# Moving the down projections' residual gain work into the up projections of a two-layer trunk

## The chip, the core and the metric

The kernel runs on one core of a Trainium2 chip. The metric is the device time of one execution in microseconds. A core has five engines, each with a queue that it works through in order: TensorE (PE, matmuls; its weight loads are shown as PEld), VectorE (DVE), ScalarE (ACT), GpSimd (POOL) and SyncE (SP), which here does nothing but issue DMAs. ACT and POOL issue some DMAs too. Engines wait for each other and for DMAs through semaphores, and so does the issue of a DMA: an entry in SP's queue whose buffer is not free yet holds up all entries behind it.

## The reference

All is float32, one sequence of 1024 rows, model width 1024, two layers. Layer 0's mixer is a gated delta net, layer 1's is retention. A layer is

```python
y = mixers[i](x * (1.0 + sc1) + sh1)
x = layer_norm(DN_ALPHA * x + (1.0 + g1) * y, ln_g[i, 0], ln_b[i, 0])
y = conv_ffn(x * (1.0 + sc2) + sh2, ffn_up[i], ffn_conv_w[i], ffn_conv_b[i], ffn_down[i])
x = layer_norm(DN_ALPHA * x + (1.0 + g2) * y, ln_g[i, 1], ln_b[i, 1])
```

with `conv_ffn` = (silu(causal conv of width 3 over `h @ up_gate`) * (`h @ up_value`)) @ `ffn_down`, hidden width 2816. The vectors sh, sc, g come from `e @ ada_w[i] + ada_b[i]`, e being a projection of the condition.

What matters here is the `x` in the fourth line. It is the normalized row times `ln_g[i, 0]` plus `ln_b[i, 0]`. The kernel stores the third line's rows without this scale and shift, since the matmul path folds them into its own scale and shift (`fold`), and applies them apart for the residual of the fourth line: one multiply and one add over each of 8 row tiles of 128 x 1024.

## The kernel before

**Matmuls.** Each float32 matmul is done as three passes on split operands (high and low part, `split`, lines 89 and 90: ACT makes the high part, DVE subtracts to get the low part; for a few tiles POOL subtracts). The large products use Strassen-Winograd with seven block products (`strassen` for the up projections, `proj_gen` for layer 1's output projection and for both down projections). An FFN runs so: the up projection's two first items with ordinary products (`side`), in between `build_T` and its `rest` make the sums and differences of input blocks on DVE; then 20 items by `wino`, each with seven products whose weight blocks DVE combines (L1217) and splits; two weight loads per item (L1223, L1224) into two `wr` buffers. Gate and value meet in `conv` and `gated` (L1563 to L1582), POOL makes four sums per pair of tiles (L1589), and SP stores them (L1573). The down projection then goes through seven products of eleven blocks each; per block SP loads one activation block (`ar`, L1274) and one weight block (`Br`, `Bw`, L1307), ACT and DVE split both. Its products p are, in this order: 11, S1 T1, S2 T2, S4 22, 12 21, S3 T3, 22 T4.

**Background work.** `bg_step` runs queued units (twice per `wino` item, once per down projection block): the `ada_w` vectors (`bg_ada`: a load `mvw` at L215, then DVE's L225 and L227), and `bg_gain`, which does the scale and shift for the residual of layer 1's mixer output on POOL (L397, L398) during retention.

**The residual of the down projections.** Layer i's rows after the mixer lie in DRAM as `xs[0]` and `xs[2]`, stored by ACT's queue (`ln_store`, L374). In `proj_gen`, four row tiles of the first half are loaded (`xload`, L284) during product p = 2, and DVE multiplies and adds in place (L1357, four operations of 128 x 512 per tile). For the second half, `gain_half` runs eight times during p = 3 and 4: SP loads 128 x 512 of a row tile into one of two `xT` buffers (L1347), POOL multiplies and adds (L1349), and POOL's own queue stores the result to DRAM, `xg[i + 1]` (L1350). These rows come back with `xload` before the last product. The scale and shift rows are broadcast over 128 partitions by `gain_rows` into four of the eight `auh` buffers, which later hold retention's `trig` tables (L1636).

**What sets the order.** The program is written as a stream and put in order per engine when it is built, by a planner that simulates a time line and starts an operation as soon as its data and buffers allow, earlier written ones first among those that are ready. A few loads are pinned with `after(...)` to be issued behind an anchor load. So a unit's place in the source is the latest point more than the only one.

Of the kernel before, what the change touches and what calls it, by code (L numbers as in the profile page):

```python
# [12 lines left out]
ALU = mybir.AluOpType  # L13
AX = mybir.AxisListType

P = 128
# [3 lines left out]
HALF = 512  # L20
# [13 lines left out]
def trunk_kernel(ctx: ExitStack, tc, A):  # L34
# [79 lines left out]
    bg, pend = [], []  # L114
# [4 lines left out]
    def bg_step(tile=mm_tile):  # L119
        bg_ps[0] = tile  # L120
        for p in pend:
            p[0] -= 1
        while pend and (pend[0][0] <= 0 or not bg):
            pend.pop(0)[1]()
            if not bg:
                break
        if bg:
            nxt = bg.pop(0)()
            if nxt:
                pend.append(list(nxt))  # L130

    def gemm_feat(src, hT_, step=True):
        w = load_w(src)
# [244 lines left out]

    xg = [dr.tile([S, D], F32, tag=f"xg{i}", name=f"xg{i}") for i in range(3)]

    def bg_gain(n, src, dst):
        gb = []

        def unit(c, r):
            if r == 0:
                gb[:] = [tl("auh", [P, HALF], name="gb") for _ in range(2)]
                for t, nm in zip(gb, ("ln_g", "ln_b")):
                    sp.dma_start(t, A[nm][n:n + 1, hs(c)].to_broadcast([P, HALF]))
            x = tl("lane", [P, HALF], name="xg")
            rs = slice(r * P, r * P + P)  # L390
            sp.dma_start(x, src[rs, hs(c)])
            if r == 7:
                return gain(x, rs, c)
            return 1, lambda: gain(x, rs, c)

        def gain(x, rs, c):
            pool.tensor_tensor(x, x, gb[0], ALU.mult)  # L397
            pool.tensor_tensor(x, x, gb[1], ALU.add)  # L398
            sp.dma_start(dst[rs, hs(c)], x)

        for c in range(2):
            for r in range(8):
                bg.append(lambda c=c, r=r: unit(c, r))

    def ln_hooks(half, xts, tag, vecs2, out, dst, key, npool=0):
        def build(f):
# [754 lines left out]
    def strassen(hT0, xts, scale, shift, items, tags=("hTb", "hTb", "qkv", "qkv", "aux"), direct=False):  # L1161
        B = {"11": hT0[:4], "21": hT0[4:]}
        nblk = [0]
        nacc = [0]

        def mm_on(*a, **kw):
            return pe.matmul(*a, skip_group_check=True, **kw)  # L1167

        held = {}

        def side(n, s):
            out = []
            for u in items[n][:2]:
                w = held.pop(u.offset, None) or load_w(u)
                if n == 0 and s == 0:
                    held[u.offset] = w
                X = acc_tile()
                for i, b in enumerate((("11", "21"), ("12", "22"))[s]):
                    for k in range(4):
                        mm3(X, w, k + 4 * i, B[b][k], i == 0 and k == 0, i == 1 and k == 3)  # L1180
                out.append(X)
            return out

        ahead, sinks = {}, {}
        for n in (1, 0):
            X = side(n, 0)
            if direct:
                sinks[n] = items[n][2]()
                for i in range(2):
                    sinks[n](2 * i, X[i], None)  # L1190
                continue
            ahead[n] = [tl("cv", [P, 516], name="ah")[:, 0:HALF] for _ in range(2)]
            for t, x in zip(ahead[n], X):
                act.activation(t, x, AF.Copy)
        rest = build_T(B, xts, scale, shift, tags)

        def block(src):
            n = nblk[0]
            nblk[0] += 1
            t = tl(("wh", "wl")[n % 2], [P, 2, HALF], F32R, name="wb")  # L1200
            split(t[:, 0], t[:, 1], src)
            return kn(t[:, 0]), kn(t[:, 1])

        def prod(src, b, onto=None):
            w = block(src)
            if onto is None:
                nacc[0] += 1
                acc = (acc_tile, acc_tile, sc_tile)[nacc[0] % 3]()
            else:
                acc = onto  # L1210
            for k in range(4):
                mm3(acc, w, k, B[b][k], onto is None and k == 0, k == 3, mm_on if onto is not None else pe.matmul)
            return acc

        def psub(x, y, op=ALU.subtract):
            t = mm_tile()
            dve.tensor_tensor(t, x, y, op)  # L1217
            return t

        def wino(n, sink):  # L1220
            ua, ub = items[n][:2]
            wa, wb = tl("wr", [P, D]), tl("wr", [P, D])
            sp.dma_start(wa, ua)  # L1223
            sp.dma_start(wb, ub)  # L1224
            a11, a12, a21, a22 = wa[:, hs(0)], wa[:, hs(1)], wb[:, hs(0)], wb[:, hs(1)]
            def copy_of(X, tag="cv"):
                t = tl(tag, [P, 516] if tag == "cv" else [P, HALF], name="pc")[:, 0:HALF]
                act.activation(t, X, AF.Copy)  # L1228
                return t

            X = prod(a11, "11")
            p1 = copy_of(X)
            s1 = psub(a21, a22, ALU.add)
            sink(0, prod(a12, "21"), p1)
            s2 = psub(s1, a11)
            Z = prod(s1, "T1")
            z5 = copy_of(Z)
            s4 = psub(a12, s2)
            prod(s2, "T2", X)
            u2 = copy_of(X)  # L1240
            s3 = psub(a11, a21)
            prod(s4, "22", Z)
            sink(1, Z, u2)
            bg_step()
            prod(s3, "T3", X)
            u3 = copy_of(X, "t2")
            sink(3, X, z5)
            sink(2, prod(a22, "T4"), u3)
            bg_step()

        bg_tag[0] = "lane"
        for n in range(2):
            if not direct:
                sinks[n] = items[n][2]()
                for i in range(2):
                    sinks[n](2 * i, ahead[n][i], None)
            X = side(n, 1)
            for i in range(2):
                sinks[n](2 * i + 1, X[i], None)
            if n == 0:  # L1260
                rest()
            if items[n][3]:
                items[n][3]()
        for n in range(2, len(items)):
            wino(n, items[n][2]())
            if items[n][3]:
                items[n][3]()
        bg_tag[0] = "wr"
        return B
# [5 lines left out]
            return raw  # L1275
        return ablk

    def proj_gen(nj, ablk, wsrc, slots, xsrc, G, final, ln_next, tag, ltags, dst, key, mm=pe.matmul, gate=None, gain=None):
        bal = {nm: BAL[ltags[4] + nm] for nm in ABLK + ("w11", "w21", "w22", "wT1", "wT2", "wT3", "wT4", "n", "h")}
        pa = [tl("aux", [P, 2, HALF], name="pa") for _ in range(4)]  # L1280
        p1 = [pa[t // 2][:, t % 2] for t in range(4)]
# [56 lines left out]

        xts = [[], []]
        stats = [[], []]  # L1340
        grows = gain_rows(gain[0], key) if gain else None

        def gain_half(n):
            hf, rs = n // 4, slice(HALF + n % 4 * P, HALF + (n % 4 + 1) * P)
            x = tl("xT", [P, HALF], name="xg")
            with after("w"):
                sp.dma_start(x, gain[1][rs, hs(hf)])  # L1347
            for r, op in zip(grows, (ALU.mult, ALU.add)):
                pool.tensor_tensor(x, x, r[hf], op)  # L1349
            pool.dma_start(xsrc[rs, hs(hf)], x)  # L1350

        def xload(half, t):
            xt = load_row(xsrc if half or not gain else gain[1], half, t)
            if half == 0 and gain:
                for r, op in zip(grows, (ALU.mult, ALU.add)):
                    for hf in range(2):
                        dve.tensor_tensor(xt[:, hs(hf)], xt[:, hs(hf)], r[hf], op)  # L1357
            xts[half].append(xt)
            stats[half].append(tl("st", [P, 2, 6]))

        def finish(half, t, nh, c):
# [89 lines left out]
        for p, (an, bn, fin, side, fresh) in enumerate(prods):  # L1451
# [8 lines left out]
            for j in range(nj):  # L1460
# [5 lines left out]
                with after("a"):  # L1466
                    for st in steps[p * nj + j + ahead:p * nj + j + ahead + 1]:
                        load_b(*st)
                if gain and p in (3, 4) and j % 2 == 0 and j < 8:
                    gain_half((p - 3) * 4 + j // 2)  # L1470
                if gain and p == 2 and j % 2 == 0 and j < 8:
                    xload(0, j // 2)
                if p == 2 and j < 4 and gate:
                    xload(0, j)
# [44 lines left out]
    def layer_tail(i, mix, wout, xsrc, x_mid, x_out, ln_next, final):  # L1519
# [11 lines left out]
        else:  # L1531
            mix.append((sc2, sh2))
            hT0, xts = proj_st(mix[0])
        bg_ada(i, 5, "row")
        if i == 0:
            for j in (1, 0, 4, 3):
                bg_ada(1, j, "col")
# [5 lines left out]
        def pair_items(fp):  # L1543
# [31 lines left out]
            def up_start():  # L1575
                seen = []

                def gated(q, a, b):
# [7 lines left out]
                    if len(seen) == 4:  # L1586
# [6 lines left out]
            return [(up[4 * fp], up[4 * fp + 2], gate_start, conv), (up[4 * fp + 1], up[4 * fp + 3], up_start, None)]  # L1593

        strassen(hT0, xts, sc2, sh2, [it for fp in range(NF // 2) for it in pair_items(fp)])
        slots = {"c": "hTa", "x": "qkv"}
        gb2 = gain_rows(3, ("mid", i), "hTb") if final else None
        return proj_st(proj_gen(NF // 2, ablk_of(ad, "qkv"), A["ffn_down"][i], slots, xg[i + 1], rows[i, 5],
                       (gb2, x_out) if final else None, ln_next, "hTb", ("hTb", "hTa", 8, 6, "f") if final else ("qkv", "hTa", 8, 4, "0"), x_out, ("out", i), gain=(2 * i, x_mid)))

    g1 = two("auh", F32, "g1")
    for nh in range(2):
# [355 lines left out]
```

## Time and profile before

| | |
|---|---|
| runs | 2961.66, 2965.21, 2967.01 us; median 2965.21 |
| profiled execution | 2955.5 us; its span 2953.7 us |
| mean granted TensorE clock | 0.984 |
| busy share | PE 95%, PEld 78%, DVE 76%, ACT 45%, POOL 15% |
| layer 0: mixer output projection ends, up projection begins | about 747 us |
| layer 0: up projection to down projection | about 1200 us |
| layer 1: mixer output projection ends, up projection begins | about 2275 us |
| layer 1: up projection to down projection | about 2727 us |

In a row of a group: line of the kernel, engine, operation, what is written <- what is read, shape, count, then total busy us and mean ns of one, then idle us of the engine just before and what ended it. In a row of a timeline: start and duration in us, engine (with q for its queue: issuing a DMA), line, operation, tiles, count; in brackets the idle time of the engine before it and what ended it. In a row of stretches: from:to and length, then busy us and count per engine, granted clock, DMA share and GB/s.

### The profile page before, as it was taken

What the parts mean: (1) busy time and instruction counts of PE and PEld (TensorE: products, weight loads), DVE (VectorE), ACT (ScalarE), POOL (GpSimd) and SP (SyncE); (2) the same over time, 40 slices, a digit from 0 to 9 for tenths busy, and PEclk for the clock granted to TensorE, in tenths of its full rate; (3) what the DMA queues carried; (4) which work ended last, traced back from release to release, by engine and by line L of the source; (5) the groups of instructions that cost most, each with busy time, mean ns of one, the idle gap of its engine ahead of it and who ended that gap; (6) DMA issues with size and microseconds to landing.
All of it is one profiled execution on the core that took longest, in us unless ns stands there. A gap on an engine that the chain in (4) does not pass through costs nothing.

```text
span 2953.7 us, 38896 instructions
## 1 busy us (share of the span) xinstructions
PE 2816.4 (95%) x13638; PEld 2303.2 (78%) x13638; DVE 2243.3 (76%) x4005; ACT 1318.0 (45%) x2413; POOL 451.1 (15%) x469
## 2 busy tenths in 40 slices
PE   8998898999999999999999999999999899999997
PEld 7887777887788888877878877777777788888885
DVE  5788787656688888968676756666689787777989
ACT  4745565444544444545333333222244544445443
POOL 0302221100001111140000022422202011111211
PEclk9999999999999999999999999999999999999999
DMA  7231222254244445765343364755654343324763
GB/s 277 86 111 65 83 79 80 83 168 158 92 160 163 150 162 174 286 225 175 131 147 121 109 229 144 222 169 177 198 204 146 103 136 107 107 102 159 278 205 136
DMA packets 244403, 451.01 MB, mean 153 GB/s; under 512 B 23088, under 2 KB 76592, under 8 KB 244208
## 3 DMA queue, kind: packets, MB, share of 16 engines
q1 hardware_dynamic: 213088, 401.07, 41.1%
q10 hardware_dynamic: 29760, 43.00, 4.0%
q0 software_dynamic: 1360, 4.46, 0.4%
q8 instruction: 107, 1.75, 0.2%
q14 instruction: 88, 0.72, 0.1%
HBM read 339.91 MB, written 108.53 MB: 152 GB/s over the span
## 4 chain that ended last, share of the span: by engine, by line
PE 77%; DVE 9%; DMA 6%; ACT 4%; issue 2%; POOL 1%; SPq 0%; POOLq 0%; ACTq 0%; DVEq 0%
PE acc L655 15%; PE acc L1167 10%; PE acc L110 6%; PE acc L111 6%; PE acc L112 6%; PE sc L1167 5%; PE acc L1441 4%; PE sc L655 4%; PE mm L655 2%; PE sc L111 2%; PE sc L112 2%; PE sc L110 2%; PE mm L658 1%; DMA Br<-in_ffn_down 1%; PE acc L314 1%
## 5 line engine op out<-in xcount | busy, mean ns | idle before, releaser
L655 PE MATMUL acc<-hT,wh 128*128 128x512 f32 x960 | 300.1, 394 | 0.0
L1441 PE MATMUL acc<-bb,ab 128*128 128x512 f32 x984 | 233.4, 395 | 9.7 <-DVE bb L90 7.0
L1589 POOL TENSOR_TENSOR o<-o 128x512 f32<-128x512 f32 x80 | 112.3, 1414 | 793.6 <-DVE o L1582 494.0
L1441 PEld LDWEIGHTS acc<-bb,ab 128*128 128x128 f32 x984 | 183.7, 189 | 54.0 <-DVE bb L90 11.8
L1167 PE MATMUL acc<-T,wb 128*128 128x512 f32 x840 | 202.9, 390 | 6.5 <-DVE wb L90 6.5
L655 PEld LDWEIGHTS acc<-hT,wh 128*128 128x128 f32 x960 | 182.2, 190 | 34.1
L89 ACT ACTIVATE ab<-ar 128x512 fp32r<-128x512 f32 x210 | 130.4, 627 | 174.1 <-PE mm L291 57.4
L655 PE MATMUL acc<-hT,wl 128*128 128x512 f32 x480 | 201.2, 419 | 0.0
L1167 PEld LDWEIGHTS acc<-T,wb 128*128 128x128 f32 x840 | 157.0, 188 | 42.9 <-DVE wb L90 9.8
L90 DVE TENSOR_TENSOR wl<-wr,wh 128x1024 fp32r<-128x1024 f32 x95 | 123.3, 1298 | 81.9 <-ACT wh L89 81.6
L90 DVE TENSOR_TENSOR ab<-ar,ab 128x512 fp32r<-128x512 f32 x210 | 159.7, 765 | 30.0 <-ACT ab L89 29.9
L90 DVE TENSOR_TENSOR wb<-mm,wb 128x512 fp32r<-128x512 f32 x216 | 146.0, 684 | 26.4 <-ACT wb L89 25.5
L89 ACT ACTIVATE wh<-wr 128x1024 fp32r<-128x1024 f32 x95 | 100.8, 1062 | 142.8 <-PE acc L655 66.4
L90 DVE TENSOR_TENSOR wb<-wr,wb 128x512 fp32r<-128x512 f32 x162 | 110.5, 687 | 69.0 <-ACT wb L89 68.8
L1228 ACT ACTIVATE pc<-acc 128x512 f32<-128x512 f32 x143 | 84.9, 594 | 163.1 <-PE acc L1167 108.8
L1568 DVE SCALAR_TENSOR_TENSOR o<-g,vc,o 128x512 f32<-128x512 f32 (+2 forms) x176 | 145.6, 844 | 6.2 <-ACT o L1563 5.5
L89 ACT ACTIVATE wb<-mm 128x512 fp32r<-128x512 f32 x216 | 123.9, 595 | 53.8 <-DVE mm L1217 49.3
L89 ACT ACTIVATE wb<-wr 128x512 fp32r<-128x512 f32 x162 | 99.8, 629 | 99.7 <-DMA wr<-in_ffn_up 36.4
L655 PE MATMUL acc<-wh,hT 128*128 128x512 f32 x384 | 137.4, 420 | 2.9 <-DVE vv L90 1.7
L110 PE MATMUL acc<-T,wb 128*128 128x512 f32 x292 | 115.6, 396 | 9.4 <-DVE wb L90 9.4
L476 DVE SCALAR_TENSOR_TENSOR qkv<-raw,vc,qkv 128x512 f32<-128x512 f32 x144 | 111.7, 780 | 11.4 <-ACT qkv L474 10.7
L111 PE MATMUL acc<-T,wb 128*128 128x512 f32 x292 | 115.1, 394 | 0.0
(641 smaller groups left out, 7428.6 us busy)
## 6 DMA issues: line engine op xcount, KB each, us to landing
wr<-in_ffn_up SPq DMA_DIRECT2D x92, 512.0 KB, 4.2
mvw<-in_ada_w SPq DMA_DIRECT2D x80, 512.0 KB, 4.1
ad<-o SPq DMA_DIRECT2D x154, 256.0 KB, 3.1
ar<-ad SPq DMA_DIRECT2D x154, 256.0 KB, 4.8
Br<-in_ffn_down SPq DMA_DIRECT2D x88, 256.0 KB, 4.3
wr<-in_ret_wv SPq DMA_DIRECT2D x32, 512.0 KB, 4.1
ar<-od SPq DMA_DIRECT2D x56, 256.0 KB, 5.4
xs<-xt ACTq DMA_DIRECT2D x24, 512.0 KB, 3.6
```

What stands on the lines that cost most here:

```text
L89: act.activation(dst_h, src, AF.Copy)
L90: eng.tensor_tensor(dst_l, src, dst_h, ALU.subtract)
L110: mm(acc, wl[:, k], hl[0], start=first, stop=False)
L111: mm(acc, wh[:, k], hl[1], start=False, stop=False)
L112: mm(acc, wh[:, k], hl[0], start=False, stop=last)
L476: dve.scalar_tensor_tensor(oh, raw[:, 3 - j:515 - j], w[:, 3 - j:4 - j], oh, ALU.mult, ALU.add)
L655: pq(pe.matmul(out, lhsT, rhs, start=start, stop=stop), cost)
L1167: return pe.matmul(*a, skip_group_check=True, **kw)
L1228: act.activation(t, X, AF.Copy)
L1441: return pe.matmul(*args, skip_group_check=True, **kw)
L1568: dve.scalar_tensor_tensor(tv, gv[:, c0 - j:c1 - j], w[:, 2 - j:3 - j], tv, ALU.mult, ALU.add)
L1589: (dve if fp == 0 else pool).tensor_tensor(o[d], o[x], o[y], op)
```

## The change

The scale and shift of the residual rows, of both halves, become sixteen units of `bg_gain` per layer with buffers of the tag `xT` in place of `lane`. They go into a queue of their own (`rowq`), of which `row_step` takes one per `wino` item, in the up projection: load on SP, multiply and add on POOL with the next step, store to `xg[i + 1]` on POOL's queue. The down projection loses `gain_half` and DVE's four operations per tile, and loads both halves from `xg[i + 1]`. The gain rows take two `auh` buffers per half width in turn, not four at once.

```diff
+    rowq, rowp = [], []
+
+    def row_step():
+        if rowp:
+            rowp.pop()()
+        if rowq:
+            nxt = rowq.pop(0)()
+            if nxt:
+                rowp.append(nxt[1])
...
-    def bg_gain(n, src, dst):
+    def bg_gain(n, src, dst, tag="lane"):
...
-            x = tl("lane", [P, HALF], name="xg")
+            x = tl(tag, [P, HALF], name="xg")
...
-            sp.dma_start(dst[rs, hs(c)], x)
+            (sp if tag == "lane" else pool).dma_start(dst[rs, hs(c)], x)
...
-                bg.append(lambda c=c, r=r: unit(c, r))
+                (bg if tag == "lane" else rowq).append(lambda c=c, r=r: unit(c, r))
...
             sink(2, prod(a22, "T4"), u3)
             bg_step()
+            row_step()
...
-        grows = gain_rows(gain[0], key) if gain else None
-
-        def gain_half(n):
-            hf, rs = n // 4, slice(HALF + n % 4 * P, HALF + (n % 4 + 1) * P)
-            x = tl("xT", [P, HALF], name="xg")
-            with after("w"):
-                sp.dma_start(x, gain[1][rs, hs(hf)])
-            for r, op in zip(grows, (ALU.mult, ALU.add)):
-                pool.tensor_tensor(x, x, r[hf], op)
-            pool.dma_start(xsrc[rs, hs(hf)], x)
 
         def xload(half, t):
-            xt = load_row(xsrc if half or not gain else gain[1], half, t)
-            if half == 0 and gain:
-                for r, op in zip(grows, (ALU.mult, ALU.add)):
-                    for hf in range(2):
-                        dve.tensor_tensor(xt[:, hs(hf)], xt[:, hs(hf)], r[hf], op)
-            xts[half].append(xt)
+            xts[half].append(load_row(xsrc, half, t))
...
-                if gain and p in (3, 4) and j % 2 == 0 and j < 8:
-                    gain_half((p - 3) * 4 + j // 2)
-                if gain and p == 2 and j % 2 == 0 and j < 8:
+                if not gate and p == 2 and j % 2 == 0 and j < 8:
                     xload(0, j // 2)
...
         bg_ada(i, 5, "row")
+        bg_gain(2 * i, x_mid, xg[i + 1], "xT")
...
         strassen(hT0, xts, sc2, sh2, [it for fp in range(NF // 2) for it in pair_items(fp)])
+        while rowq or rowp:
+            row_step()
```

More of the change, by code (lines that the diff above doesn't have):

```diff
@@ L1276, in ablk_of, with proj_gen @@
         return ablk
-    def proj_gen(nj, ablk, wsrc, slots, xsrc, G, final, ln_next, tag, ltags, dst, key, mm=pe.matmul, gate=None, gain=None):
+    def proj_gen(nj, ablk, wsrc, slots, xsrc, G, final, ln_next, tag, ltags, dst, key, mm=pe.matmul, gate=None):
         bal = {nm: BAL[ltags[4] + nm] for nm in ABLK + ("w11", "w21", "w22", "wT1", "wT2", "wT3", "wT4", "n", "h")}
@@ L1598, in layer_tail @@
         return proj_st(proj_gen(NF // 2, ablk_of(ad, "qkv"), A["ffn_down"][i], slots, xg[i + 1], rows[i, 5],
-                       (gb2, x_out) if final else None, ln_next, "hTb", ("hTb", "hTa", 8, 6, "f") if final else ("qkv", "hTa", 8, 4, "0"), x_out, ("out", i), gain=(2 * i, x_mid)))
+                       (gb2, x_out) if final else None, ln_next, "hTb", ("hTb", "hTa", 8, 6, "f") if final else ("qkv", "hTa", 8, 4, "0"), x_out, ("out", i)))
     g1 = two("auh", F32, "g1")
```

## The prediction

> **What bounds the kernel now.** I read the page's span, busy shares and chain first, then sums by stretch of time, then the timelines of the places that the change touches.
>
> ```profile
> span 2953.7 us, 38896 instructions
> PE 2816.4 (95%) x13638; PEld 2303.2 (78%) x13638; DVE 2243.3 (76%) x4005; ACT 1318.0 (45%) x2413; POOL 451.1 (15%) x469
> PE 77%; DVE 9%; DMA 6%; ACT 4%; issue 2%; POOL 1%; SPq 0%; POOLq 0%; ACTq 0%; DVEq 0%
> ```
>
> TensorE (PE) is busy 95% and makes 77% of the chain, so work taken from VectorE (DVE) or GpSimd (POOL) is worth only the PE waits that it ends. By stretch (us, then busy time and count of PE, PEld, DVE, ACT, POOL, then clock and DMA): layer 0's down projection, the part of it in which the residual rows get their gain, the same part of layer 1, and the openings of both up projections.
>
> ```profile
> 1200.00:1440.00 240.00, 228.38 (x1012) 186.78 (x1011) 196.30 (x311) 112.95 (x193) 48.29 (x36) 0.99 0.66 226
> 1230.00:1314.00 84.00, 84.00 (x373) 69.54 (x372) 61.64 (x83) 38.99 (x68) 34.93 (x24) 1.00 0.69 237
> 2750.00:2840.00 90.00, 90.00 (x399) 74.53 (x398) 72.80 (x98) 43.42 (x76) 30.46 (x24) 1.00 0.71 242
> 785.00:811.00 26.00, 20.62 (x90) 16.30 (x88) 22.94 (x34) 15.27 (x25) 0.00 (x0) 0.98 0.18 61
> 2313.30:2339.30 26.00, 20.64 (x90) 16.30 (x88) 22.94 (x34) 15.24 (x25) 0.00 (x0) 0.99 0.18 61
> ```
>
> While the gain work runs, PE is busy 84.00 of 84.00 and 90.00 of 90.00 us. In the openings PE has gaps, DVE is busy 22.94 of 26 us and POOL does nothing.
>
> **What is removed.** By line, both in the down projections:
>
> ```profile
> L1357 DVE TENSOR_TENSOR xt<-xt,rowb 128x512 f32<-128x512 f32 x32 | 20.8, 681 | 0.0
> L1349 POOL TENSOR_TENSOR xg<-xg,rowb 128x512 f32<-128x512 f32 x32 | 56.0, 1749 | 126.2 <-DMA xg<-xs 124.9
> ```
>
> DVE's 20.8 us lie beside a PE that doesn't wait: worth 0 by themselves. What counts is a queue, in layer 0 (timelines of SP, POOL, DVE, PE; start, duration, idle time before in brackets; the last row is layer 1's PE at the same step):
>
> ```profile
> 1302.58 0.38 SPq L1274 DMA_DIRECT2D ar<-ad  x1
> 1306.42 0.33 SPq L1636 DMA_DIRECT2D trig<-in_trig  x1
> ...
> 1309.54 0.46 SPq L1307 DMA_DIRECT2D Br<-in_ffn_down  x1
> ...
> 1305.12 2.65 POOL L1349 TENSOR_TENSOR xg<-xg,rowb 128x512 f32<-128x512 f32 x2 [0.78 <-DMA xg<-xs]
> ...
> 1314.80 0.69 DVE L1321 TENSOR_TENSOR Br<-Bw,Br 128x512 f32<-128x512 f32 x1 [10.19 <-DMA Br<-in_ffn_down]
> ...
> 1322.24 0.77 PE L289 MATMUL sc<-bb,ab 128*128 128x512 f32 x1 [6.98 <-DVE u L1414]
> 1322.80 0.63 PE L290 MATMUL sc<-bb,ab 128*128 128x512 f32 x1
> ...
> 2842.22 0.47 PE L289 MATMUL sc<-bb,ab 128*128 128x512 f32 x1 [0.74 <-DVE u L1414]
> ```
>
> SP's in-order queue stands from 1302.96 until POOL's last multiply with the old gain row ends (1306.4), because a `trig` load takes that row's buffer. The `Br` behind it leaves at 1309.54, DVE idles 10.19 us, PE 6.98. Layer 1 has the same gain work but no `trig`, and loses 0.74. Without gain work SP stands on nothing here: **-7.0**, with **-1.3** for the matmuls that restart slowly (0.77 and 0.63 long where layer 1's took 0.47; an estimate over six of them), and **-0.7** in layer 1. Late next is `Br` itself, which DVE reads first. Gain: -9.0; bounds -5 (half of the wait is taken by another one) and -12 (nearly the whole 11.6 us that PE idles in the stage). The gain rows are loaded in the same number, four per layer: 0.
>
> **Where the work goes.** The built program's order, which holds no time, shows that the sixteen row steps of a layer are not spread over the up projection. Nothing in their data holds them back, so all stand at its opening, and before it. SP's queue in layer 1 (u0 to u15 are the row loads):
>
> ```
> ar<-od, xg u0, xg u1, wr, xg u2, xt<-xg x4, xg u3, wr x4, xg u4, wr,
> xg u5 to u11, wr (L1223), wr (L1224), xg u12 to u15, mvw<-in_ada_w
> ```
>
> POOL's: multiply u0, the `hT` split, add u0, multiply u1, store u0, add u1, store u1, and so on. Two `xT` buffers carry the steps, so u2's load waits for u0's store, and all that stands behind it on SP waits too. Per layer there are 16 loads, 32 operations and 16 stores, 8, 16 and 8 more than before. All are done before POOL's first `L1589`, so the body of the up projections stays as it is: 0.
>
> How POOL and DVE get on, from two places, and what hangs on it (timelines of POOL, DVE, ACT, PE):
>
> ```profile
> 1253.14 10.30 POOL L1349 TENSOR_TENSOR xg<-xg,rowb 128x512 f32<-128x512 f32 x2 [42.48 <-DMA xg<-xs]
> ...
> 2247.47 7.58 POOL L90 TENSOR_TENSOR hT<-t,hT 128x512 fp32r<-128x512 f32 x1 [5.18 <-ACT hT L89]
> ...
> 1262.21 1.78 DVE L90 TENSOR_TENSOR bb<-Bw,bb 128x512 fp32r<-128x512 f32 x1
> ...
> 2253.25 0.69 DVE L1362 TENSOR_TENSOR pa<-pa,rowb 128x512 f32<-128x512 f32 x1
> ...
> 2255.09 0.78 ACT L272 ACTIVATE t<-mm,fh,fs 128x512 f32<-128x512 f32 x1 [5.25 <-POOL hT L90]
> ...
> 2255.92 0.44 PE L270 MATMUL mm<-cst,xt 128*128 128x128 f32 x2 [3.27 <-ACT t L272]
> ```
>
> A POOL operation of 1.3 us (2.65 for two, above) took 7.58: it got in only when DVE's unbroken stream ended at 2253.94, and was done 1.1 us later. Where POOL does get in, DVE's 0.68 becomes 1.78: 1.1 us lost per meeting.
>
> [...]
>
> *Layer 1, end of the mixer's output projection* (timelines, DMA groups with median us to landing, DVE alone in one stretch):
>
> ```profile
> 2240.96 0.34 ACTq L374 DMA_DIRECT2D xs<-xt  x1
> ...
> xs<-xt ACTq DMA_DIRECT2D x24, 512.0 KB, 3.6
> xg<-xs SPq DMA_DIRECT2D x32, 256.0 KB, 3.7
> xg<-xg POOLq DMA_DIRECT2D x16, 256.0 KB, 3.2
> mvw<-in_ada_w SPq DMA_DIRECT2D x80, 512.0 KB, 4.1
> ...
> 2257.10:2262.50 5.40, 5.40 (x9) 0.69 0.02 4
> ...
> 2261.50 1.76 SPq L284 DMA_DIRECT2D xt<-xg  x4
> ...
> 2265.28 0.69 DVE L1364 SCALAR_TENSOR_TENSOR xt<-xt,pa 128x512 f32<-128x512 f32 x1 [1.71 <-DMA xt<-xg]
> ...
> 2275.46 0.50 PE L110 MATMUL acc<-hT,wl 128*128 128x512 f32 x1 [0.93 <-DVE xt L1364]
> ```
>
> First, u0's row is stored at 2240.96, landed at 2244.6, loaded by 2248.3. Its multiply stands ahead of `hT` on POOL and takes the turn at 2253.94; `hT` follows 1.3 us later, and behind it ACT, PE and DVE: **+1.3** (0 to 2.3, one or two meetings). Second, u0's store stands behind u1's multiply, which meets DVE's next unbroken stream (5.40 of 5.40 us, ending near 2263.8 with the shift). That multiply ends near 2265, the store goes at 2265.3 and lands about 3 later. Only then do u2 and the four `xt<-xg` leave SP, near 2268.3 in place of 2261.50 + 1.3. DVE already waited for them (1.71) and PE for DVE (0.93), so nothing covers it: **+5.5**. If POOL gets in between two DVE operations it is 0 to 2.2; if DVE's stream runs on, 8. I take the value by the row that this place is most like, the 7.58 from ten microseconds before.
>
> *Openings of the up projections* (PE, DVE and SP timelines):
>
> ```profile
> 811.14 0.80 PE L110 MATMUL acc<-T,wb 128*128 128x512 f32 x1 [4.69 <-DVE wb L90]
> 2339.46 0.79 PE L110 MATMUL acc<-T,wb 128*128 128x512 f32 x1 [4.69 <-DVE wb L90]
> 811.01 0.48 DVE L225 TENSOR_SCALAR ada<-mvw,e 128x512 f32<-128x512 f32 x1
> 751.11 10.88 SPq L102 DMA_DIRECT2D wr<-in_ffn_up  x3
> ...
> 1256.16 0.42 SPq L1347 DMA_DIRECT2D xg<-xs  x1
> ...
> 1273.19 0.32 SPq L1347 DMA_DIRECT2D xg<-xs  x1
> ```
>
> PE already waits 4.69 us for DVE there. One turn of a buffer is load 3.7, two operations 2.65, gap 0.3, store 3.2: 9.9 us for two steps, so ten or eleven POOL operations fall into each 26 us. If half meet DVE, that is 5.5 x 1.1 = 6, of which the 3.06 us that DVE is free take about one: **+5** in layer 0 and **+5** in layer 1 (each 0 to 12). The weights for L1223 and L1224 stand behind u10 and u11 by a microsecond or so, within what PE waits anyway. Behind u15 stands the `mvw` load that DVE's L225 needs. In layer 0 u5 leaves by 761.7 (the last of the three weights), u15 five turns later near 811; `mvw` lands at 815.6, DVE comes to L225 at 811.01 + 5. I take **+1** (0 to 6 with turns of 11 us). In layer 0 u0 to u3 also run before, at the end of `gdn_wout`, where DVE has room: **+0.5** (0 to 3).
>
> **Sum**, against the profiled execution of 2955.5 us: -9.0 + 1.3 + 5.5 + 5 + 5 + 1 + 0.5 = +9.3, 2964.8. The median of the runs shown, 2965.2, is 9.7 above that execution; on it the forecast is **2974.5**.
>
> **Rivals.**
> *Faster.* POOL falls beside DVE's PSUM readings and idle time in the openings, and u1's multiply gets in at once: only the 1.3 is left of the costs, -7.7, 2957.5. For it: DVE's free 3.06 us, and `hT`'s kind of wait is rare. Against it: 22.94 of 26 busy. It decides when the costs stay under 3 us.
> *Washed out.* POOL gets its turn between DVE operations at the end of layer 1's mixer (2.2 in place of 5.5), and the openings lose half as much: -9.0 + 1.3 + 2.2 + 2.5 + 2.5 + 1 + 0.5 = +1.0, 2966.2. For it: the 1.78 row.
> *Much slower.* The turns take as long as between the last two rows above, 1256.16 to 1273.19, 17 us: u15 leaves at 847, `mvw` lands at 851, 35 us after DVE wants it, +43 in all: 3009. Against it: DMA is at 0.18 in the opening, and DVE has breaks. [...]
>
> **How the numbers follow.** About 6 us (0.2%) is what a measurement of this kernel can tell from no change. Forecast 0.55, its own range 2971 to 2989 (+6 to +24); faster 0.20, washed out 0.18, much slower 0.07. Faster by over 0.2%: 0.20; within: 0.18; slower: 0.62. The range, 2957 to 2997, takes in the faster case and the openings' upper bounds, and leaves out the much slower one.
>
> **What would show it.** Right: PE's wait near 1322 falls under 1 us and DVE's 10.19 is gone; POOL's first multiply of layer 1 takes over 5 us with `hT` behind it; `xt<-xg` leaves SP five or more us later against its PE neighbours; the waits at 811 and 2339 grow from 4.69 to 8 or more. Wrong: those two waits unchanged (the meetings cost nothing), `xt<-xg` not behind u0's store, or a new `Br` wait at 1322 that eats the gain.

## The result, and the profile after

The changed kernel takes 2976.71 us (median of 7 runs, 2969.08 to 2982.94), the kernel before 2964.14 beside it (7 runs, 2953.20 to 2967.28): 12.6 us more, a ratio of 1.0044 with an interval of 1.0028 to 1.0060. The forecast was 2974.5. That it lies so near is luck: the cost was forecast too small and so was the gain, as the traces and the experiments below show.

The page of the changed kernel (span, busy shares, chain by engine):

```profile
span 2974.9 us, 38976 instructions
PE 2822.2 (95%) x13638; PEld 2309.1 (78%) x13638; DVE 2234.3 (75%) x3973; ACT 1317.1 (44%) x2413; POOL 512.7 (17%) x517
PE 27%; DVE 6%; DMA 3%; POOL 1%; issue 1%; ACT 0%; SPq 0%; POOLq 0%; DVEq 0%; ACTq 0%
```

POOL has 61.6 us more, DVE 9 less although it lost 20.8 us of operations, and PE does the same work in a span that is 21.2 us longer. The chain of this execution is followed only over part of the span (its shares add up to 38%), so I go by single steps instead. The changed kernel's PE at steps that the two kernels share, by the timeline:

```profile
724.51 0.79 PE L324 MATMUL acc<-wh,hl 128*128 128x512 f32 x1 [1.70 <-DVE t L354]
731.29 0.51 PE L324 MATMUL acc<-wh,hl 128*128 128x512 f32 x1 [1.72 <-DVE t L354]
...
827.80 0.80 PE L110 MATMUL acc<-T,wb 128*128 128x512 f32 x1 [13.88 <-DVE wb L90]
...
1332.29 0.39 PE L299 MATMUL sc<-bb,ab 128*128 128x512 f32 x1
...
1367.43 0.74 PE L1437 MATMUL acc<-bb,ab 128*128 128x512 f32 x2 [1.43 <-DVE bb L90]
...
2271.26 1.11 PE L280 MATMUL mm<-cst,xt 128*128 128x128 f32 x4 [6.31 <-ACT t L282]
...
2365.30 0.80 PE L110 MATMUL acc<-T,wb 128*128 128x512 f32 x1 [8.85 <-DVE wb L90]
```

The prediction's rows have four of them before, at 811.14 [4.69], 1322.24 [6.98], 2255.92 [3.27] and 2339.46 [4.69]. The fifth, by the timeline of the profiled execution before:

```profile
1360.30 0.98 PE L1441 MATMUL acc<-bb,ab 128*128 128x512 f32 x3 [2.87 <-DVE bb L90]
```

The wait near 1322 is gone (VectorE's waits there are 1.43 at most, where one was 10.19), the waits of both openings have grown to 13.88 and 8.85, that at the end of layer 1's mixer to 6.31. But the difference of the two spans, 21.2, is far more than the 12.6 of the medians. A second profiled execution of the kernel before:

> The kernel before, unchanged, for a second profiled execution. The first one (2955.5 us) lies about 8 us below the median of the kernel's runs, and the changed kernel's (2976.7 us) on its median, so the two traces differ by 21 where the medians differ by 12.6. Theory: what varies is the wait of layer 0's down projection near 1322, which was 13.34 in the slow execution of e3_trig_late: an execution at 2962 or more shows it at 10 us or more. Rival: that wait stays at 7 us and the difference is spread over the rest (retention above all).

It took 2967.61 us. Its span and the same steps:

```profile
span 2965.8 us, 38896 instructions
...
811.80 0.79 PE L110 MATMUL acc<-T,wb 128*128 128x512 f32 x1 [4.69 <-DVE wb L90]
...
1333.95 0.76 PE L289 MATMUL sc<-bb,ab 128*128 128x512 f32 x1 [16.49 <-DVE u L1414]
...
1372.01 1.20 PE L1441 MATMUL acc<-bb,ab 128*128 128x512 f32 x4 [1.70 <-DVE bb L90]
...
2271.03 1.03 PE L270 MATMUL mm<-cst,xt 128*128 128x128 f32 x4 [3.27 <-ACT t L272]
...
2354.39 0.79 PE L110 MATMUL acc<-T,wb 128*128 128x512 f32 x1 [4.69 <-DVE wb L90]
```

That wait is 16.49 here and 6.98 in the first execution; the openings and the mixer's end are alike to 0.01. The theory holds for these two: of the 12.1 us between them 9.5 are this wait. It isn't all that varies, though. The two executions of e3_trig_late further down, one kernel, lie 15.5 us apart with 3.3 of it in this wait; 9.8 lie in retention, which took 904.0 and 894.2 us there (from the step near 1360 to the end of layer 1's mixer).

The changed kernel less the kernel before, by stage (differences of the starts quoted, then of the spans):

| stage, up to | against the first execution | against the second |
|---|---|---|
| the wait that ends layer 0's opening | +16.7 | +16.0 |
| the step after layer 0's gain work (1360) | -9.5 | -20.6 |
| end of layer 1's mixer | +8.2 | +4.8 |
| the wait that ends layer 1's opening | +10.5 | +10.7 |
| the end | -4.6 | -1.8 |
| all | +21.2 | +9.1 |

The medians' 12.6 lies between. Of the third row 3.04 is the wait of 6.31 against 3.27; the rest, 5 and 2 us, is spread over retention, where the two executions of the kernel before differ from each other by 3.4 (2255.92 - 1360.30 against 2271.03 - 1372.01), so I don't count it as the change's.

### The profile page after: what moved, and what is told of

Read it like the earlier page. It is cut to its first block, busy times and chain, and to the rows that moved or that the text cites. A ratio compares the mean times of both kernels' runs of the same rounds, so it can differ in the third digit from the quotient of the medians.

```text
span 2974.9 us, 38976 instructions
## 1 busy us (share of the span) xinstructions
PE 2822.2 (95%) x13638; PEld 2309.1 (78%) x13638; DVE 2234.3 (75%) x3973; ACT 1317.1 (44%) x2413; POOL 512.7 (17%) x517
## 5 line engine op out<-in xcount | busy, mean ns | idle before, releaser
L1584 POOL TENSOR_TENSOR o<-o 128x512 f32<-128x512 f32 x80 | 126.0, 1586 | 691.6 <-DVE o L1577 457.0
L1177 PE MATMUL acc<-T,wb 128*128 128x512 f32 x840 | 203.0, 390 | 5.8 <-DVE wb L90 5.7
L90 DVE TENSOR_TENSOR ab<-ar,ab 128x512 fp32r<-128x512 f32 x210 | 147.2, 706 | 58.8 <-ACT ab L89 58.8
L407 POOL TENSOR_TENSOR xg<-xg,gb 128x512 f32<-128x512 f32 x48 | 75.2, 1567 | 416.7 <-ACT wb L89 274.2
L110 PE MATMUL acc<-T,wb 128*128 128x512 f32 x292 | 115.7, 396 | 22.8 <-DVE wb L90 22.7
```

The costliest lines, as they stand in the source:

```text
L90: eng.tensor_tensor(dst_l, src, dst_h, ALU.subtract)
L110: mm(acc, wl[:, k], hl[0], start=first, stop=False)
L1584: (dve if fp == 0 else pool).tensor_tensor(o[d], o[x], o[y], op)
```

## The experiments

**The openings: is it the operations?** Three kernels leave the steps where the change puts them and alter only what POOL does in them; each takes one of the three lines below in place of the two that go.

```diff
 def gain(x, rs, c):
-    pool.tensor_tensor(x, x, gb[0], ALU.mult)
-    pool.tensor_tensor(x, x, gb[1], ALU.add)
+    # nothing for tag "xT"                                               # e2_no_ops
+    for _ in range(5): pool.memset(x, 0.0)                              # e4_fill
+    for _ in range(2): pool.tensor_scalar(x, x, 1.0, None, ALU.mult)    # e8_one_in
```

> The changed kernel without GpSimd's multiplication and addition of the 32 residual row halves (the loads and stores stay, so the residual rows go without scale and shift: that part of the computation is left out). Theory (the operations themselves cost the time): most of the 29 us go, 2950 to 2957. Rival (the loads in SP's queue, and the weights behind them, cost it): the turn of a buffer falls only from about 10 to 7 us, and the time stays at 2968 to 2978.

> The changed kernel with the two GpSimd operations of a row step replaced by five fills of the same tile, which write and read nothing (an estimate of 0.5 us each, so that a step is about as long; the residual rows become zero: scale, shift and the rows' own values are left out). Theory (GpSimd's operations cost by taking their operands over what VectorE reads with): about as e2_no_ops, 2950 to 2958. Rival (what costs is the length of a step: the buffers' turn, SP's queue behind it and the operations queued on GpSimd): 2970 to 2978, as the changed kernel.

> The changed kernel with the two GpSimd operations of a row step replaced by two that read one tile in place of two (a multiplication by the number 1: scale and shift of the residual rows are left out). Theory (only GpSimd operations that read two tiles in SBUF take the reading over from VectorE): as e2_no_ops and e4_fill, 2950 to 2957. Rival (any reading operation of GpSimd takes it): 2966 to 2977, near the changed kernel.

Measured: e2_no_ops 2954.81 (ratio to the kernel before 0.9976, interval 0.9959 to 0.9993), e4_fill 2951.61 (0.9968, 0.9951 to 0.9984), e8_one_in 2954.68 (0.9969, 0.9954 to 0.9984). All three are 8 to 11 us below the kernel before where the change is 12.6 above, as the three theories had it: without the two-input operations the time is 20 to 24 us less, though five fills keep POOL nearly as long (an estimate of 2.6 us a step from 0.53 each, where the two operations took 3.0). The intervals overlap, so the three are not told apart.

The steps are not free without these operations, though. By the starts of the same PE steps (from 723.18 to 849.43 us and from 2255.92 to 2377.76 us in the first execution before), the openings have grown by:

| kernel | layer 0 | layer 1 |
|---|---|---|
| the changed kernel | 15.3 | 10.5 |
| e2_no_ops | 3.3 | 5.5 |
| e4_fill | 5.2 | 5.2 |
| e8_one_in | 4.1 | 3.4 |

Two PE waits of e2_no_ops and one wait of DVE in e4_fill:

```profile
814.91 0.79 PE L110 MATMUL acc<-T,wb 128*128 128x512 f32 x1 [8.04 <-DVE wb L90]
...
2340.40 0.80 PE L110 MATMUL acc<-T,wb 128*128 128x512 f32 x1 [8.06 <-DVE wb L90]
```

```profile
828.41 1.29 DVE L1588 TENSOR_TENSOR o<-o 128x512 f32<-128x512 f32 x2 [4.97 <-DMA ad<-o]
```

In e2_no_ops ACT, which splits the weights behind the row loads ahead of DVE, waits 11.5 us for these loads from 785 to 846 us (4.3 before); in e4_fill the stores behind the row loads come late. In the changed kernel DVE is late itself by then and waits for neither. So leaving out the two-input operations takes 10 to 12 of layer 0's 15.3 us away and 5 to 7 of layer 1's 10.5; what stays hangs on SP's queue at the places shown.

DVE's groups by form from 785 to 846 us, first of the kernel before, then of the changed kernel, e8_one_in (with POOL's group) and e4_fill:

```profile
L90 DVE TENSOR_TENSOR T<-bt,T 128x512 fp32r<-128x512 f32 x11 | 7.2, 687 | 1.3 <-ACT T L89 1.3
L454 DVE TENSOR_TENSOR bt<-bt,mm 128x512 f32<-128x512 f32 x3 | 2.0, 681 | 0.0
```

```profile
L90 DVE TENSOR_TENSOR T<-bt,T 128x512 fp32r<-128x512 f32 x15 | 16.6, 1136 | 1.4 <-ACT T L89 1.4
L464 DVE TENSOR_TENSOR bt<-bt,mm 128x512 f32<-128x512 f32 x3 | 2.0, 679 | 0.0
```

```profile
L412 POOL TENSOR_SCALAR xg<-xg 128x512 f32<-128x512 f32 x16 | 26.4, 1653 | 18.8 <-DMA xg<-xs 18.3
L90 DVE TENSOR_TENSOR T<-bt,T 128x512 fp32r<-128x512 f32 x13 | 10.9, 878 | 1.4 <-ACT T L89 1.4
```

```profile
L90 DVE TENSOR_TENSOR T<-bt,T 128x512 fp32r<-128x512 f32 x13 | 8.5, 688 | 2.0 <-ACT T L89 2.0
```

On average over this stretch the same subtraction takes 687 ns alone, 1136 with two-input operations, 878 with one-input ones and 688 with fills. Where one of DVE's two inputs comes from PSUM (`bt<-bt,mm`) it isn't slowed, 681 and 679, although all three of the changed kernel run beside an operation of POOL. The theory of e8_one_in is met in its time but not in its reason: one-input operations slow DVE too, only less (878 against 687), and fills, which read nothing, don't (688).

How many meetings there are, by stretches around layer 0's opening, from one PE step to another that the two kernels share (414 matmuls), and around layer 1's; first the kernel before, then the changed one (PE, PEld, DVE, ACT, POOL):

```profile
728.00:829.00 101.00, 94.39 (x414) 75.77 (x413) 71.36 (x118) 50.48 (x77) 3.65 (x4) 0.97 0.33 113
2275.00:2339.30 64.30, 57.89 (x264) 46.30 (x264) 49.31 (x81) 32.79 (x54) 3.97 (x4) 1.00 0.23 82
```

```profile
731.00:846.00 115.00, 94.62 (x414) 75.41 (x415) 91.82 (x122) 51.02 (x78) 46.51 (x40) 0.94 0.53 179
2288.00:2365.30 77.30, 61.81 (x275) 48.77 (x273) 65.82 (x85) 34.35 (x55) 47.29 (x43) 0.95 0.44 154
```

DVE is 20.5 and 16.5 us busier over four more operations each. In the timeline of the changed kernel 19 operations of DVE in layer 0's opening (768 to 826 us, with 24 of POOL) and 14 in layer 1's (2288 to 2365) are longer than their kind was before, most by 1.0 to 1.1 us, 18 and 14 us together. PE takes 14 us longer over the same 414 matmuls, and 13 longer over 275 in place of 264.

**The steps spread over the body, as the source reads.**

```diff
-            sp.dma_start(wb, ub)
+            anchor["row"] = sp.dma_start(wb, ub)
...
+            with after("row" if tag == "xT" else None):
                 sp.dma_start(x, src[rs, hs(c)])
```

> The changed kernel with each row step tied behind the weight load of the feed-forward item in which the code calls it, so that one step falls into each of sixteen items of the up projection's body, none into its opening, none into the end of the projection before it. Theory (the costs are GpSimd operations that meet VectorE in the two openings and at the two projections' ends, about 13.5 + 11.4 + 1.9 + 2 = 29 us by the traces, and the down projections still gain about 10): 2953 to 2957, that is 8 to 11 us below the kernel before. Rival (the body has no more room than the opening: each of the 64 operations costs PE there as much as it did in the opening, about 0.4 us): 2970 to 2980, no better than the changed kernel.

2959.57 (0.9990, 0.9975 to 1.0004): 3.1 below the kernel before, which isn't told apart from no change, and some 16 better than the change. Neither expectation holds. The openings' waits are back to 5.73 and 5.80, but layer 0's body, which ran without a PE wait worth naming, now loses about 9 us by the starts of the same PE steps (811 to 1203 us before). One group of DVE in the body, before and in e1_paced:

```profile
L90 DVE TENSOR_TENSOR wb<-wr,wb 128x512 fp32r<-128x512 f32 x52 | 35.6, 686 | 7.2 <-ACT wb L89 7.2
```

```profile
L90 DVE TENSOR_TENSOR wb<-wr,wb 128x512 fp32r<-128x512 f32 x52 | 39.5, 759 | 8.2 <-ACT wb L89 8.1
```

Here too operations with two SBUF inputs grow, from 686 to 759 ns, while `wb<-mm,wb`, with one input from PSUM, stays at 684 and 683 over 71 of them. The body has less room than I thought, more than the opening.

**Layer by layer.** The change in one layer, with `gain_half` and its DVE operations kept in the other.

```diff
+        if i == 0:            # e11_layer0; i == 1 in e12_layer1
+            bg_gain(2 * i, x_mid, xg[i + 1], "xT")
...
-    ("out", i)))
+    ("out", i), gain=(2 * i, x_mid) if i else None))    # None if i else ... in e12_layer1
```

> The change in layer 0 alone: layer 1 takes its gain in the down projection, as the kernel before. Theory (layer 0 pays about 13.5 + 1.9 in the opening and ahead of it, and is given back its wait near 1322, 7 to 16.5 and some more; layer 1 pays about 11.4 + 2 and is given back 2.3): between -3 and +6 against the kernel before, 2960 to 2968, so that most of the 12.6 is layer 1's. Rival (the loss is shared by the layers, or is layer 0's by its larger opening): +7 to +13, 2970 to 2976.

> The change in layer 1 alone: layer 0 takes its gain in the down projection, as the kernel before. Layer 0 alone was 7.2 below the kernel before, all of the change 12.6 above it. Theory (the layers add up, and layer 1's down projection gives little back): the rest is layer 1's, +18 to +21, 2981 to 2986 against 2963 to 2965. Rival (the traces: the opening's 11.4, 2 at the end of the mixer, 2.3 given back): +9 to +13, 2973 to 2977, and then the two parts alone don't add up to the whole.

Layer 0 alone: 2957.93, 7.2 below the kernel before (0.9981, 0.9970 to 0.9993). Layer 1 alone: 2980.65, 17.0 above (1.0052, 1.0034 to 1.0070). Together +9.8, and the interval of the whole change (+8 to +18 us) holds that. The first is 2 us below the range of its theory, the second 0.4 below that of its own and 3.7 above the rival's, with an interval (+10 to +21 us) that tells neither apart: layer 1 carries the whole loss, since little comes back there, while layer 0 pays its opening with the wait near 1322. The waits are reproduced: e11_layer0's opening, then e12_layer1's mixer end and its opening.

```profile
825.70 0.80 PE L110 MATMUL acc<-T,wb 128*128 128x512 f32 x1 [12.78 <-DVE wb L90]
```

```profile
2273.84 1.11 PE L280 MATMUL mm<-cst,xt 128*128 128x128 f32 x4 [6.30 <-ACT t L282]
...
2371.55 0.80 PE L110 MATMUL acc<-T,wb 128*128 128x512 f32 x1 [9.80 <-DVE wb L90]
```

From the mixer's end to this step e12_layer1 takes 97.7 us, where the kernel before takes 83.5 and the changed kernel 94.0: 14.2 more than before in this execution.

**What the wait near 1322 is.** The prediction laid it on the `trig` loads. Four edits of the kernel before:

```diff
+                    with after("w"):                          # e3, e3b, e5, e9: trig late
                         sp.dma_start(t[hf], (A["trig"][i] if j else A["trigq"][h, i])[:, hs(hf)])
...
-                if gain and p in (3, 4) and j % 2 == 0 and j < 8:
-                    gain_half((p - 3) * 4 + j // 2)
+                if gain and p in (1, 2, 3, 4) and j in (0, 4):  # e5: spread
+                    gain_half((p - 1) * 2 + j // 4)
...
-"xT": 2}
+"xT": 3}                                                       # e9, e10: three buffers
```

> The kernel before with one edit: the trig loads are held back behind the weight loads that are traced before them, so that SP has none of them in layer 0's down projection. The gain work stays there. Theory (the 6.98 us wait at 1322 is SP standing behind trig for the old gain row): that wait falls under 1.5 us and the time is 6 to 9 us below the kernel before. Rival (GpSimd's gain work starves the stage in another way too, and the next wait takes over): within 3 us of the kernel before.

> The kernel of e3_trig_late once more, since the profiled execution there was its slowest one of twelve (2967.5 against a median of 2955.9). Theory (trig is one of several loads that SP holds back for the gain work, and what is left varies with the landing of the row loads): the wait near 1322 is under 5 us in an execution at 2956 or less. Rival (trig has nothing to do with it): 7 us or more there in any execution.

> The kernel before with two edits: the trig loads held back as in e3_trig_late, and the eight gain steps of a down projection put one into every four or six of its items over four of its seven products, in place of one into every two items over two products. Theory (SP stands behind a row load until GpSimd is done with the step before the last, and the weights behind it come late): with double the time per step SP doesn't stand, no wait of over 2 us is left near 1322, and the time is 2948 to 2954. Rival (trig was all of it): as e3_trig_late, 2955 to 2958. Second rival (the earlier steps meet VectorE where it has less room): 2960 or more.

> The kernel before with the trig loads held back, as in e3_trig_late, and three xT buffers in place of two, so that a row load (and the mvw load that takes the same buffers) need not wait for the store of the step before the last. Theory (the wait near 1322 comes from SP standing at the loads into the two xT buffers, 7 to 16.5 us in the executions seen, and trig is the smaller part): the wait falls under 4 us and the time is 2945 to 2953. Rival (what is late is GpSimd itself, held up by VectorE, so a third buffer only moves the queue): the wait stays at 6 us or more and the time at 2954 to 2958.

> The kernel before with three xT buffers and nothing else; the trig loads stand where they stood. Theory (buffers are the larger part of the wait): 2950 to 2957. Rival (trig, which waits for GpSimd's last use of the old gain row, is as long whatever the buffers): 2959 to 2964.

| kernel | edit | us | ratio to before, interval | the wait, in an execution of (us) |
|---|---|---|---|---|
| e3_trig_late | trig late | 2955.88 | 0.9981, 0.9965 to 0.9997 | 13.34 (2967.54) and, in e3b_trig_late, 10.04 (2952.01) |
| e5_spread | trig late, steps spread | 2955.00 | 0.9978, 0.9965 to 0.9991 | 6.57 (2962.44) |
| e10_three_only | three buffers | 2956.03 | 0.9965, 0.9953 to 0.9977 | 8.44 (2960.84) |
| e9_three | trig late, three buffers | 2951.84 | 0.9953, 0.9940 to 0.9966 | 2.04 (2951.82) |

With `trig` out of the way the kernel is 6.8 us faster, as the theory of e3 had it, and yet the wait is there at 10.04 and 13.34: the expectation of under 5 failed, and so did the thought that `trig` is all of it. SP's waits from 1238 to 1335 us, in the second execution before, in e3b_trig_late and in e9_three (total us, times, longest), and PE's wait of the latter two:

```profile
SPq L1347 <- DMA xg<-xg: 24.7, 4, 10.7
...
SPq L1636 <- POOL xg L1349: 7.6, 3, 4.3
...
SPq L215 <- DMA xg<-xg: 2.3, 2, 1.5
```

```profile
SPq L1347 <- DMA xg<-xg: 24.6, 4, 9.8
...
SPq L215 <- DMA xg<-xg: 9.3, 2, 6.2
...
1324.95 0.77 PE L289 MATMUL sc<-bb,ab 128*128 128x512 f32 x1 [10.04 <-DVE u L1414]
```

```profile
SPq L1347 <- DMA xg<-xg: 12.1, 3, 8.4
SPq L215 <- DMA xg<-xg: 4.6, 2, 3.2
...
1321.58 0.77 PE L289 MATMUL sc<-bb,ab 128*128 128x512 f32 x1 [2.04 <-DVE u L1414]
```

SP stood 24.7 us for the stores of earlier steps, so that a row load could have one of two `xT` buffers, and 7.6 us for `trig`. Without `trig`, the next in line, the `mvw` loads of retention, stood 9.3 us for the same stores. A third buffer halves the longer waits; with both edits 2.04 is left, and the theories of e9_three and e10_three_only hold. The wait is not the same thing as the time, though: e3b_trig_late and e9_three took 2952.01 and 2951.82 with 10.04 and 2.04 of it. Spreading the steps shows nothing over holding `trig` back, and its theory, that SP would not stand, is wrong: one row load there stood 27 us. e3's edit takes 6.8 us, e10's 9.1 and both together 13.3, which agrees with two causes whose parts nearly add up.

**e9_three beats both kernels**: 13.3 us (0.45%) below the kernel before. It keeps the gain work in the down projections.

## Why the prediction was right, and where it wasn't

*Gain, layer 0 (-7.0 - 1.3).* That the wait goes is shown: no wait stands at 1332.29. Its cause was half wrong. The prediction let SP stand "because a `trig` load takes that row's buffer"; the runs show `trig` as the smaller of two, the other being the two `xT` buffers. The execution that it read shows this too (SP's waits from 1238 to 1335 us):

```profile
SPq L1347 <- DMA xg<-xg: 19.8, 4, 7.4
...
SPq L1636 <- POOL xg L1349: 8.2, 3, 3.8
```

Its size was read from one execution with 6.98, where another has 16.49; the stage gave back 9.5 against the one and 20.6 against the other. Layer 1's -0.7 is part of the -1.8 to -4.6 behind its opening.

*The step onto the median failed.* The sum was +9.3 on an execution of 2955.5 us, and 9.7 were added to come to the median. In the second execution, 12.1 longer, the wait alone is 9.5 longer, and the change takes that away whole, so it should not have been carried over. How much of the way to the median this wait makes in other executions isn't shown. On the executions compared the changed kernel is 21.2 above, not 9.3. The missing 11.9 and the carried 9.7 cancelled by luck, and left the forecast 2.2 below the measured time.

*Openings (+5, +0.5 and +5).* The mechanism, GpSimd meeting DVE at about 1.1 us a time, is right, and the fills show it (688 ns with them, 1136 with two-input operations); the number of meetings is what was mis-sized most. Layer 0 lost 16.7 to the end of its opening, with about 1.5 of that at the end of `gdn_wout` (1.70 and 1.72 against one wait of 1.91 before), and layer 1 10.5 to 10.7. The prediction counted the ten or eleven operations that fit beside the 26 us at the end, half of them in a meeting. But the steps run beside the whole of `build_T` before it as well: 24 of POOL's operations in layer 0, and 19 and 14 meetings in place of five or six each. The weights for L1223 and L1224 left SP at 795.77 and 800.56, 7.4 and 9.7 later than before, where the prediction had about one; DVE, later still, waited for neither. Its upper bound of 12 for one opening was too low for layer 0.

*The `mvw` load behind u15 (+1).* It cost nothing. By the timeline of the changed kernel (SP, DVE):

```profile
819.16 0.39 SPq L225 DMA_DIRECT2D mvw<-in_ada_w  x1
...
827.66 0.47 DVE L235 TENSOR_SCALAR ada<-mvw,e 128x512 f32<-128x512 f32 x1
```

The turns of a buffer took 10.8 us on average where the prediction worked out 9.9 (u5 left SP at 764.95, u15 at 818.75; the last turn, from u13 at 809.72, took 9.0), but DVE itself came 16.7 later than before. The "much slower" rival falls with it. POOL's 32 stores of the changed kernel took 0.59 us to issue on average and 0.76 at most, and landed in a median of 2.7 us, where the 16 before landed in 3.2.

*Layer 1, end of the mixer (+1.3 and +5.5).* Timeline of POOL, DVE and SP in the changed kernel:

```profile
2259.30 9.87 POOL L407 TENSOR_TENSOR xg<-xg,gb 128x512 f32<-128x512 f32 x1 [4.71 <-DMA xg<-xs]
...
2269.13 1.26 POOL L90 TENSOR_TENSOR hT<-t,hT 128x512 fp32r<-128x512 f32 x1
...
2271.57 1.27 POOL L407 TENSOR_TENSOR xg<-xg,gb 128x512 f32<-128x512 f32 x1
...
2271.90 1.50 DVE L90 TENSOR_TENSOR hT<-t,hT 128x512 fp32r<-128x512 f32 x1 [3.85 <-ACT hT L89]
...
2277.06 1.77 SPq L294 DMA_DIRECT2D xt<-xg  x4
```

u0's multiplication is starved as forecast, and `hT` behind it comes late: 3.04 for the 1.3, above its bound of 2.3. The second step failed. u1's multiplication was to meet DVE's next unbroken stream; it took 1.27. While POOL was starved, `hT` was missing, ACT and then DVE ran out of work, and the stream that u1 should have met began only at 2271.90, after u1's multiplication had. `xt<-xg` left at 2277.06, where 2261.50 plus the 15.3 by which PE was late is 2276.8: 0 in place of +5.5. The delay was counted twice, once as `hT`'s and once as if DVE ran on in spite of it.

*Removed DVE operations (0).* e9_three agrees: there they stay, and 2.04 is left of the wait near 1322, so they can make no more of it than that. No run takes them out alone.

*Rivals.* "Faster" and "washed out" needed openings under 3 and 5 us; layer 0's loss alone decides against them. In layer 0 by itself, though, the time fell (-7.2): not because the opening cost nothing, but because the wait that it pays with is often longer than in the execution that the prediction read: 16.49 in the second one, and 17.27 in e12_layer1, whose layer 0 is that of the kernel before, against 6.98.

## What to carry to other kernels

Before a wait is priced from one profile, see how far that execution lies from the median: where it lies off, the wait in question may be what varies (6.98 and 16.49 us here), and then the difference belongs to the term and not to the base. A second profile of the same kernel tells. Work moved to GpSimd isn't free because GpSimd is idle (beside it a VectorE subtraction took 1136 ns on average here, 687 without); count the VectorE operations with two SBUF inputs in the whole stretch in which the moved work can run, which a planner may put earlier than the source reads. When an in-order DMA queue stands, take all the waits in it: with `trig` held back the `mvw` loads stood 9.3 us in place of 2.3, and a third buffer for the ring that they wait for, one character here, was worth 9.1 us where holding the load back was worth 6.8.

## What the runs showed of the hardware that I had not expected

GpSimd operations with one SBUF input slow VectorE's two-input subtractions far less than those with two (878 against 1136 ns on average from 785 to 846 us, 687 alone), though they take no less time themselves (1.65 us each over 16, against 1.52 over the 32 of layer 0 in the changed kernel), and fills don't at all (688).

A GpSimd operation that came into an unbroken stream of VectorE's was done only 1.1 us after its end (2269.17 against 2268.05, layer 1 of the changed kernel), 9.87 us for 1.3, while operations of VectorE that started later went ahead. In the openings, where VectorE's stream is mixed with operations that read PSUM, the 128 x 512 operations of GpSimd took 2.2 us at most.

What stays open: why a row load of e5_spread could stand 27 us at so little cost, and why layer 1's opening costs 14.2 us in e12_layer1 and 10.5 in the changed kernel. With the 3.0 ahead of it, and about 2 that come back later, the 14.2 make some 15 of the 17.0.
